# Five more w1/w3 tile pairs of each feed-forward block by seven products, and the first two w2 tiles of a third merged

## The chip, the cores and the metric

The program runs on one core of one Trainium2 chip. The metric is the device time of one execution in microseconds (us), the median of several runs.

## The reference

Two blocks follow each other on a sequence of 512 positions of width 1024, each two layers deep. The first is a hybrid attention block, the second holds feed-forward, mixer, cross-attention and again feed-forward. The change touches the feed-forward blocks alone; there are two in each of the second block's layers, so four in all:

```python
D_FF = ((8 * D_MODEL // 3) + 127) // 128 * 128          # 2816 = 22 tiles of 128

def swiglu(h, w1, w3, w2):
    return (jax.nn.silu(h @ w1) * (h @ w3)) @ w2
...
    x = x + 0.5 * swiglu(rmsnorm(x, ffn1_norm[l]), ffn1_w1[l], ffn1_w3[l], ffn1_w2[l])
...
    x = x + 0.5 * swiglu(rmsnorm(x, ffn2_norm[l]), ffn2_w1[l], ffn2_w3[l], ffn2_w2[l])
```

## The kernel before

Everything is kept transposed: channels on the 128 partitions, the 512 positions along the free axis. Each fp32 operand is split into a high part, a ScalarE copy rounded to fp32r (line L284 for weights), and a low part, VectorE's difference (L285); a product of two split operands is three matmuls on TensorE (`mm3`, L313 to L315: high by high, low by high, high by low).

A feed-forward block (`ffn`, L1059) works through its 22 hidden tiles in three thirds of 8, 7 and 7. A third has two stages.

**The pair stage.** For each hidden tile one unit computes the columns of h @ w1 and of h @ w3, applies silu and multiplies. There are two kinds of units. `gated_pair` (L917), the plain one, multiplies 16 weight blocks of 128x128 by 512 positions: 48 matmuls of 512 columns. `seven` (L951) treats the pair as a 2x2 block product over w1 and w3's halves and the positions' halves, and needs seven block products in place of eight: 7 x 4 x 3 = 84 matmuls of 256 columns. In exchange VectorE builds sums of weights (`sums`, L962), splits more weight tiles (L285: three of 1024 columns and one of 512, against two of 1024 for a plain unit), and combines the products out of PSUM (tiles `early` and `ab`, also L962). The string `PLAIN` (L33) says by a 1 which units of a third are plain.

The four weight splits of a unit of seven are called p0 to p3 in the code; the text below calls them a, s, t and d after the names under which they are kept. The products come in the order m1, m2, m6, m5, m7, m3, m4. Split s is first read by the third of them (m6), t by the fifth (m7) and d by the seventh (m4). After m4, VectorE's last add (`early<-mm,ab`) completes the unit, GpSimd multiplies by the norm's factor (L1038), ScalarE takes the silu (L1039), VectorE multiplies the halves (L1040, `sb<-early,sb`), and the result is split into `hh` and `hl` for the second stage: `hh` by ScalarE (L1073), `hl` either by VectorE (L1078, plain units and the last two of a third) or by a ScalarE copy and an accumulating DMA from GpSimd's queue (L1075, L1076).

Split weight tiles share one pool of eight buffers, so four pairs of high and low part:

```python
        return [self._new(self.sb, [P, 1040], R, "w", 8, "w" + e)[:, :n] for e in "hl"]
```

Since a unit of seven fills all four pairs, split a of the next unit waits until this unit's m2 has read its a, s until m5, t until m3, d until m4.

**The w2 stage.** For each of the 8 output tiles, one unit of `dense` multiplies the third's hidden tiles (7 or 8 blocks, three matmuls of 512 columns each) and adds into x (L1101, L1102). `go` (L408) runs the units one after another, so the first unit reads all `hh` and `hl`, that of the last hidden tile included, before the second unit starts.

The order within each engine's queue is fixed when the program is built, by a scheduler that moves instructions of later steps forward; on the chip each queue runs in that order.

Of the kernel before, what the change touches and what calls it, by code (L numbers as in the profile page):

```python
# [29 lines left out]

THIRDS = (8, 7, 7)

PLAIN = ("11100100", "0010010", "0010010")  # L33
EPS = 1e-6
BIG = 1e30
DEPTH = 2
# [1 line left out]
GRAIN = 2  # L38
# [174 lines left out]
class Prog:  # L213
# [194 lines left out]
    def go(self, units):  # L408
        for _, f in self.parts_of(units):
            f()  # L410

    def weave(self, main, fill, keep=0, lead=0):

        self.go(fill[:lead])
        fill = fill[lead:]
        tm, tf = sum(c for c, _ in main) or 1, max(1, sum(u.cost for u in fill) - keep)
        a = b = i = 0
        for c, f in self.parts_of(fill):
            while i < len(main) and a / tm <= b / tf:
                a += main[i][0]  # L420
                main[i][1]()
                i += 1
            f()
            b += c
        for _, f in main[i:]:
            f()
# [632 lines left out]
    def ffn(self, l, name, cur, nx):  # L1059
        nc, A = self.nc, self.A  # L1060
        self.run_late()
        xs = cur.xs
        r = self.norm(cur, wait=6)
        self.later(6, lambda: self.tc.keep_in_program_order(nc.scalar.preload_act_table_set("silu_and_others")))
        w13 = A[f"{name}_w13"][l]
        mv = []
        for third, nh in enumerate(THIRDS):
            hid = {}
            j0 = sum(THIRDS[:third])

            def done(j, b, added):
                hh, hl = self.s(R, "hh"), self.s(R, "hl")
                nc.scalar.activation(hh, b, AF.Copy)  # L1073
                if added:
                    nc.scalar.activation(hl, b, AF.Copy, scale=-1.0)  # L1075
                    nc.gpsimd.dma_start(out=hl, in_=b, accum_op=ALU.add)  # L1076
                else:
                    nc.vector.tensor_tensor(hl, b, hh.bitcast(F32), op=ALU.subtract)  # L1078
                hid[j] = hh, hl

            units = []
            for j in range(nh):
                flat = w13[j0 + j].rearrange("p b k c -> p (b k c)")
                if PLAIN[third][j] == "1":
                    prep, steps = self.gated_pair(flat, xs, r, lambda b, j=j: done(j, b, False))
                    if third == 0 and j < 2:

                        def operands(f, i):
                            f()
                            mv.append(self.seven_operands(xs, f"{name}_g{l}", i))  # L1090

                        for n, at in enumerate((3, 6)):
                            steps[at] = lambda f=steps[at], i=2 * j + n: operands(f, i)
                    units.append((prep, steps))
                else:
                    units.append(self.seven(flat, mv, r, lambda b, j=j: done(j, b, j < nh - 2)))

            def ev2(m, ps):

                t = self.s(nm="xr")  # L1100
                nc.vector.scalar_tensor_tensor(t, ps, 0.5, r["r"], op0=ALU.mult, op1=ALU.mult)  # L1101
                nc.vector.tensor_tensor(self.x[m], t, self.x[m], op=ALU.add)  # L1102
                if third == 2:
                    self.ready(nx, m)

            w2 = A[f"{name}_w2"][l]
            last = self.dense([w2[i][:, j0:j0 + nh] for i in range(KD)], nh, 128, hid, ev2, quick=third == 2)
            self.run_pairs(units, last[0].prep)
            self.flush()
            if third == 2:  # L1110
                self.tc.keep_in_program_order(nc.scalar.preload_act_table_set("natural_log_exp_and_others"))
            self.go(last)
            self.flush()

    def lower_bound(self):
# [475 lines left out]
```

## Time and profile before

| | |
|---|---|
| runs shown | 2951.25 us median of 3 (2950.77 to 2956.36) |
| profiled execution, its own time | 2955.5 us |
| its span, first to last instruction | 2953.7 us |
| TensorE busy | 97% of the span |
| VectorE busy | 71% |
| ScalarE busy | 50% |
| GpSimd busy | 18% |
| mean granted TensorE clock | 0.993 of full |

The profiled execution took 1.8 us more than its span, and 4.25 us more than the median of the runs shown. Busy shares are means over all stages: an engine with a low mean can still be nearly full in one of them.

### The profile page before, as it was taken

How to read it: one execution, taken by the hardware profiler on the slowest of the kernel's cores; microseconds unless marked ns; L12 is line 12 of the kernel's file. 1: busy time of each engine (PE TensorE's matmuls, PEld its weight loads, DVE VectorE, ACT ScalarE, POOL GpSimd, SP SyncE). 2: the span in 40 equal slices, each digit the busy share in tenths (PEclk: the TensorE clock that was granted, in tenths of full speed). 3: DMA queues.
4: the chain of work that ended last, by engine and by line, in shares of the span. 5: the costliest groups of instructions: out<-in, count | busy, mean ns of one | idle time of the engine just before them, and what ended most of it. 6: DMA issues, size and time to landing. Idle time of an engine off the chain costs nothing. (4 is left out here: it accounts for less than half of the span.)

```text
span 2953.7 us, 44940 instructions
## 1 busy us (share of the span) xinstructions
PE 2871.5 (97%) x17560; PEld 2425.6 (82%) x17560; DVE 2089.3 (71%) x3354; ACT 1487.6 (50%) x2406; POOL 539.1 (18%) x445
## 2 busy tenths in 40 slices
PE   8999999999999999999999999999999899999997
PEld 6777877778789887788888988888988788888896
DVE  7876578774867667785676666766767975686674
ACT  6776467774634344464453434534345554453333
POOL 3101131011111013331010112101124331100112
PEclk9999999999999999999999999999999999999999
DMA  5432234322243342232133434334342232233432
GB/s 161 130 97 83 93 97 120 86 87 92 79 118 101 107 116 89 68 124 99 64 92 101 117 99 120 93 94 122 100 118 80 79 127 87 68 94 104 117 103 69
DMA packets 95045, 294.92 MB, mean 100 GB/s; under 512 B 12832, under 2 KB 13232, under 8 KB 94832
## 3 DMA queue, kind: packets, MB, share of 16 engines
q1 hardware_dynamic: 88752, 281.26, 30.9%
q0 software_dynamic: 5792, 10.50, 2.0%
q8 instruction: 138, 2.26, 0.3%
q14 instruction: 75, 0.61, 0.1%
q10 hardware_dynamic: 288, 0.28, 0.0%
HBM read 261.46 MB, written 2.10 MB: 89 GB/s over the span
## 5 line engine op out<-in xcount | busy, mean ns | idle before, releaser
L284 ACT ACTIVATE wh<-wraw 128x1024 fp32r<-128x1024 f32 (+3 forms) x494 | 489.2, 991 | 488.8 <-PE mm L314 357.9
L313 PE MATMUL mm<-xsh,wh 128*128 128x512 f32 (+1 forms) x1856 | 699.5, 377 | 18.2 <-ACT xsh L267 11.6
L285 DVE TENSOR_TENSOR wl<-wraw,wh 128x1024 fp32r<-128x1024 f32 (+3 forms) x494 | 572.6, 1160 | 176.8 <-ACT wh L284 171.6
L314 PE MATMUL mm<-xsl,wh 128*128 128x512 f32 (+1 forms) x1856 | 685.0, 369 | 6.1 <-DVE xsl L268 6.1
L315 PE MATMUL mm<-xsh,wl 128*128 128x512 f32 (+1 forms) x1856 | 683.6, 369 | 0.0
L313 PEld LDWEIGHTS mm<-xsh,wh 128*128 128x128 f32 x1856 | 352.2, 190 | 91.1 <-ACT xsh L267 13.3
L314 PEld LDWEIGHTS mm<-xsl,wh 128*128 128x128 f32 x1856 | 352.4, 190 | 63.4 <-DVE xsl L268 8.6
L315 PEld LDWEIGHTS mm<-xsh,wl 128*128 128x128 f32 x1856 | 352.2, 190 | 62.0 <-DVE wl L285 0.3
L313 PE MATMUL mm<-hh,wh 128*128 128x512 f32 x704 | 277.9, 397 | 15.1 <-ACT hh L1073 15.1
L1038 POOL TENSOR_TENSOR sb<-early,rt 128x512 f32<-128x512 f32 x56 | 111.8, 1996 | 988.3 <-DVE early L962 938.8
L314 PE MATMUL mm<-hl,wh 128*128 128x512 f32 x704 | 278.8, 396 | 0.9 <-DVE hl L1078 0.9
L315 PE MATMUL mm<-hh,wl 128*128 128x512 f32 x704 | 276.5, 393 | 0.0
L450 POOL TENSOR_TENSOR sq<-sq,sq 128x512 f32<-128x512 f32 (+1 forms) x97 | 142.3, 1467 | 624.7 <-ACT sq L447 612.8
L284 ACT ACTIVATE wh<-sums 128x1024 fp32r<-128x1024 f32 x112 | 118.6, 1059 | 179.7 <-PE mm L314 114.3
L1101 DVE SCALAR_TENSOR_TENSOR xr<-mm,rt 128x512 f32<-128x512 f32 x96 | 66.4, 692 | 164.1 <-PE mm L315 164.0
L285 DVE TENSOR_TENSOR wl<-sums,wh 128x1024 fp32r<-128x1024 f32 x112 | 136.8, 1221 | 53.5 <-ACT wh L284 53.5
L313 PEld LDWEIGHTS mm<-hh,wh 128*128 128x128 f32 x704 | 131.7, 188 | 49.9 <-ACT hh L1073 20.3
L314 PEld LDWEIGHTS mm<-hl,wh 128*128 128x128 f32 x704 | 132.2, 188 | 34.8 <-DVE hl L1078 5.6
L315 PEld LDWEIGHTS mm<-hh,wl 128*128 128x128 f32 x704 | 132.2, 188 | 31.2
L267 ACT ACTIVATE xsh<-x,prm 128x512 fp32r<-128x512 f32 x96 | 68.8, 718 | 118.3 <-DVE x L849 35.2
L1040 DVE SCALAR_TENSOR_TENSOR sb<-early,sb 128x512 f32<-128x512 f32 x56 | 38.8, 692 | 109.7 <-ACT sb L1039 109.7
L313 PE MATMUL mm<-wh,xsh 128*128 128x256 f32 (+1 forms) x384 | 113.7, 296 | 0.0
(411 smaller groups left out, 6454.5 us busy)
## 6 DMA issues: line engine op xcount, KB each, us to landing
wraw<-in_ffn_w_dram SPq DMA_DIRECT2D x208, 512.0 KB
wraw<-in_ffn_w_dram SPq DMA_DIRECT2D x64, 448.0 KB
z<-z SPq DMA_DIRECT2D x128, 128.0 KB
wraw<-in_w_out_dram SPq DMA_DIRECT2D x32, 512.0 KB
wraw<-in_w_qk_dram SPq DMA_DIRECT2D x30, 512.0 KB
hl<-sb POOLq DMA_DIRECT2D x40, 256.0 KB, 4.5
wraw<-in_w_g_dram SPq DMA_DIRECT2D x16, 512.0 KB
wraw<-in_w_gate_dram SPq DMA_DIRECT2D x16, 512.0 KB
```

The lines of the kernel that those rows point to most:

```text
L267: self.nc.scalar.activation(hi[:, :n], src, AF.Copy, scale=g)
L284: self.nc.scalar.activation(hi, src, AF.Copy)
L285: self.nc.vector.tensor_tensor(lo, src, hi.bitcast(F32), op=ALU.subtract)
L313: self.nc.tensor.matmul(ps, ah, bh, start=first and i == 0, stop=False)
L314: self.nc.tensor.matmul(ps, ah, bl, start=False, stop=False)
L315: self.nc.tensor.matmul(ps, al, bh, start=False, stop=last and i == n - 1)
L450: (eng or self.on("acc")).tensor_tensor(acc[:, :n], acc[:, :n], sq[:, :n], op=ALU.add)
L1038: self.later(3, lambda: nc.gpsimd.tensor_tensor(g, q[:, :T], r["r"], op=ALU.mult))
L1040: self.later(5, lambda: nc.vector.scalar_tensor_tensor(g, q[:, T:], -1.0, g, op0=ALU.mult, op1=ALU.mult))
L1101: nc.vector.scalar_tensor_tensor(t, ps, 0.5, r["r"], op0=ALU.mult, op1=ALU.mult)
```

## The change

Of a block's 22 units 14 were of seven; now 19 are. Only the first three units of the first third stay plain, and the other two thirds have none. So 5 units in each of 4 blocks change kind, 20 in all. Second, `lead_in` merges the first two w2 units of every third: the blocks 0 to 5 of both come first, then the remaining block or blocks of the first, then those of the second. The weight split of the second w2 unit is called before the last steps of the pair stage are flushed.

```diff
-PLAIN = ("11100100", "0010010", "0010010")
+PLAIN = ("11100000", "0000000", "0000000")
...
+    def lead_in(self, units):
+
+        a, b = units[:2]
+
+        def prep():
+            a.prep()
+            b.prep()
+
+        cut = 6 // GRAIN
+        return [self.Unit(a.cost + b.cost, a.parts[:cut] + b.parts[:cut] + a.parts[cut:] + [self.tick] + b.parts[cut:], prep)] + units[2:]
...
             self.run_pairs(units, last[0].prep)
+            last[1].prep()
             self.flush()
...
-            self.go(last)
+            self.go(self.lead_in(last))
```

The first place is VectorE's queue in the second third of the first block, from the last add of unit 3 to the last add of unit 4, both of seven. Line numbers after the change are higher by 11 (L973 is L962 of before, L1051 is L1040). Before, the unit that follows (5) was plain:

```order
L1040 SCALAR_TENSOR_TENSOR sb_2402_9692<-early_2389_9617,sb_2402_9692 128x512
L285 TENSOR_TENSOR wl_2414_9752<-wraw_2412_9749,wh_2413_9751 128x1024
L962 TENSOR_TENSOR early_2411_9746<-mm_2410_9720,cd_2409_9717 128x2x256
L962 TENSOR_TENSOR sums_2432_9870<-wraw_2426_9845 128x512
L962 TENSOR_TENSOR sums_2436_9891<-wraw_2425_9843,wraw_2426_9845 128x512
L285 TENSOR_TENSOR wl_2421_9790<-wraw_2419_9787,wh_2420_9789 128x1024
L962 TENSOR_TENSOR ab_2416_9781<-aux_2415_9755,early_2411_9746 128x512
L962 TENSOR_TENSOR sums_2432_9870<-sums_2432_9870,wraw_2425_9843 128x512
L962 TENSOR_TENSOR early_2411_9746<-aux_2415_9755,ab_2416_9781 128x256
L285 TENSOR_TENSOR wl_2428_9848<-wraw_2425_9843,wh_2427_9847 128x1024
```

Now it is of seven, and so is the one behind it:

```order
L973 TENSOR_TENSOR sums_2447_9946<-wraw_2434_9871,wraw_2435_9873 128x512
L973 TENSOR_TENSOR sums_2447_9946<-sums_2442_9911,wraw_2434_9871 128x512
L285 TENSOR_TENSOR wl_2437_9876<-wraw_2434_9871,wh_2436_9875 128x1024
L973 TENSOR_TENSOR early_2433_9868<-mm_2432_9842,cd_2431_9839 128x2x256
L1051 SCALAR_TENSOR_TENSOR sb_2424_9814<-early_2411_9737,sb_2424_9814 128x512
L285 TENSOR_TENSOR wl_2444_9915<-sums_2442_9911,wh_2443_9914 128x1024
L973 TENSOR_TENSOR ab_2439_9905<-aux_2438_9879,early_2433_9868 128x512
L973 TENSOR_TENSOR sums_2464_10042<-wraw_2457_10004 128x512
L973 TENSOR_TENSOR early_2433_9868<-aux_2438_9879,ab_2439_9905 128x256
L973 TENSOR_TENSOR sums_2464_10042<-sums_2464_10042,wraw_2456_10002 128x512
L285 TENSOR_TENSOR wl_2449_9950<-sums_2447_9946,wh_2448_9949 128x1024
L285 TENSOR_TENSOR wl_2451_9954<-wraw_2435_9873,wh_2450_9953 128x512
```

Between the same two adds there are now two half sums of unit 5 first (`sums_2447`), then splits and combining adds as before, and among them the two first half sums of unit 6 (`sums_2464`) and a fourth split; the multiplication behind the silu (`sb_2424`) has moved from the head of the piece to the fifth row.

The second place is TensorE's queue where the w2 stage of the same third begins. `mm_2459` is the first w2 unit's bank and `mm_2463` the second's; `hh_2454` and `hl_2455` are the last hidden tile. Before:

```order
L315 MATMUL mm_2459_10030<-hh_2449_9971,wl_2447_9955 128x512
L313 MATMUL mm_2459_10030<-hh_2454_10020,wh_2446_9954 128x512
L313 MATMUL mm_2463_10058<-hh_2362_9450,wh_2457_10026 128x512
L314 MATMUL mm_2459_10030<-hl_2455_10021,wh_2446_9954 128x512
L315 MATMUL mm_2459_10030<-hh_2454_10020,wl_2447_9955 128x512
L314 MATMUL mm_2463_10058<-hl_2363_9451,wh_2457_10026 128x512
L315 MATMUL mm_2463_10058<-hh_2362_9450,wl_2458_10027 128x512
L313 MATMUL mm_2463_10058<-hh_2375_9533,wh_2457_10026 128x512
L314 MATMUL mm_2463_10058<-hl_2376_9534,wh_2457_10026 128x512
```

Now, with `mm_2495` the first unit's bank, `mm_2496` the second's, and `hh_2490` and `hl_2491` the last hidden tile:

```order
L313 MATMUL mm_2496_10237<-hh_2483_10166,wh_2488_10200 128x512
L314 MATMUL mm_2496_10237<-hl_2484_10167,wh_2488_10200 128x512
L315 MATMUL mm_2496_10237<-hh_2483_10166,wl_2489_10201 128x512
L313 MATMUL mm_2495_10218<-hh_2490_10208,wh_2479_10135 128x512
L314 MATMUL mm_2495_10218<-hl_2491_10209,wh_2479_10135 128x512
L315 MATMUL mm_2495_10218<-hh_2490_10208,wl_2480_10136 128x512
L313 MATMUL mm_2496_10237<-hh_2490_10208,wh_2488_10200 128x512
L314 MATMUL mm_2496_10237<-hl_2491_10209,wh_2488_10200 128x512
L315 MATMUL mm_2496_10237<-hh_2490_10208,wl_2489_10201 128x512
```

The last hidden tile was read by the 19th matmul of the stage; now 36 matmuls on the other six tiles come ahead of it.

## Rows read from the trace of the kernel before

**Rows 1.** The page, busy us of each engine (share of the span), then its instructions.
```profile
PE 2871.5 (97%) x17560; PEld 2425.6 (82%) x17560; DVE 2089.3 (71%) x3354; ACT 1487.6 (50%) x2406; POOL 539.1 (18%) x445
```

**Rows 2.** Three stretches; busy us of each engine (instructions), PEclk is the clock share.
```profile
1010.45:1020.34 9.89, 9.89 (x85) 9.89 (x84) 6.16 (x9) 4.17 (x5) 0.00 (x0) 1.00 0.33 106
1020.34:1030.23 9.89, 9.89 (x87) 9.89 (x85) 7.50 (x10) 5.66 (x8) 2.16 (x2) 1.00 0.37 102
1030.23:1041.40 11.17, 11.17 (x51) 9.04 (x50) 9.02 (x14) 4.33 (x7) 3.67 (x2) 1.00 0.53 143
```

**Rows 3.** Timeline of PE, ends of two thirds: start us, us, then the instruction.
```profile
857.72 0.50 PE L313 MATMUL mm<-hh,wh 128*128 128x512 f32 x1 [1.12 <-ACT hh L1073]
858.45 0.51 PE L314 MATMUL mm<-hl,wh 128*128 128x512 f32 x1 [0.23 <-DVE hl L1078]
...
1085.91 0.40 PE L315 MATMUL mm<-hh,wl 128*128 128x512 f32 x1
1087.65 0.73 PE L313 MATMUL mm<-hh,wh 128*128 128x512 f32 x2 [1.34 <-ACT hh L1073]
...
1088.94 0.39 PE L314 MATMUL mm<-hl,wh 128*128 128x512 f32 x1
```

**Rows 4.** Timelines of ACT and DVE in the stretch's first unit.
```profile
1016.23 1.07 ACT L284 ACTIVATE wh<-sums 128x1024 fp32r<-128x1024 f32 x1 [1.79 <-PE aux L314]
1019.06 1.06 ACT L284 ACTIVATE wh<-sums 128x1024 fp32r<-128x1024 f32 x1 [1.76 <-PE mm L314]
...
1014.48 1.23 DVE L285 TENSOR_TENSOR wl<-wraw,wh 128x1024 fp32r<-128x1024 f32 x1 [1.94 <-ACT wh L284]
...
1017.33 1.22 DVE L285 TENSOR_TENSOR wl<-sums,wh 128x1024 fp32r<-128x1024 f32 x1 [1.02 <-ACT wh L284]
```

**Rows 5.** Timeline of DVE where it never waits.
```profile
1030.34 0.68 DVE L962 TENSOR_TENSOR sums<-sums,wraw 128x512 f32<-128x512 f32 x1
1030.94 0.41 DVE L962 TENSOR_TENSOR early<-aux,ab 128x256 f32<-128x256 f32 x1
1031.28 1.21 DVE L285 TENSOR_TENSOR wl<-wraw,wh 128x1024 fp32r<-128x1024 f32 x1
1032.41 0.68 DVE L962 TENSOR_TENSOR early<-mm,ab 128x512 f32<-128x512 f32 x1
```

**Rows 6.** Timelines of DVE, POOL and ACT behind two units' last adds.
```profile
1021.89 0.68 DVE L962 TENSOR_TENSOR early<-mm,ab 128x512 f32<-128x512 f32 x1
1024.71 0.69 DVE L1040 SCALAR_TENSOR_TENSOR sb<-early,sb 128x512 f32<-128x512 f32 x1 [2.13 <-ACT sb L1039]
1025.66 1.23 DVE L285 TENSOR_TENSOR wl<-wraw,wh 128x1024 fp32r<-128x1024 f32 x1 [0.26 <-ACT wh L284]
...
1022.72 1.29 POOL L1038 TENSOR_TENSOR sb<-early,rt 128x512 f32<-128x512 f32 x1 [49.58 <-DVE early L962]
...
1033.18 2.79 POOL L1038 TENSOR_TENSOR sb<-early,rt 128x512 f32<-128x512 f32 x1 [5.34 <-DVE early L962]
...
1024.04 0.63 ACT L1039 ACTIVATE sb<-sb 128x512 f32<-128x512 f32 x1 [1.71 <-POOL sb L1038]
1024.58 1.05 ACT L284 ACTIVATE wh<-wraw 128x1024 fp32r<-128x1024 f32 x1
...
1034.14 0.68 DVE L962 TENSOR_TENSOR sums<-sums,wraw 128x512 f32<-128x512 f32 x1
```

**Rows 7.** Timeline of DVE at a third's end.
```profile
1082.71 0.68 DVE L962 TENSOR_TENSOR early<-mm,ab 128x512 f32<-128x512 f32 x1
...
1087.63 0.69 DVE L1078 TENSOR_TENSOR hl<-sb,hh 128x512 fp32r<-128x512 f32 x1 [0.69 <-ACT hh L1073]
```

**Rows 8.** Two lines of the program: min/median/max of an instruction, and of a DMA's landing.
```profile
L1101 DVE SCALAR_TENSOR_TENSOR xr<-mm,rt x96: 677/692/695, 859.2 to 2936.1; 128x512 f32<-128x512 f32 x96
...
DMA to landing us min/median/max: 3.2/4.5/6.2
```

## The prediction

> **What bounds the kernel now.** I read the page first: TensorE is busy 97% of the span, VectorE 71% [rows 1], so TensorE sets the time and the other engines count only where it waits for them. Then the pair stage in windows. A unit of seven takes TensorE 9.89 us, twice in a row, at full clock, and a plain unit 11.17 us [rows 2]; the busy time equals the window each time, so nothing is waited for there. VectorE is busy 6.2, 7.5 and 9.0 of these: the wait-free window in which it is fullest is the plain one, where it works for the units of seven on either side.
>
> Then the ends of the thirds in TensorE's timeline. The w2 stage runs 18 matmuls and stops for the last hidden tile, first for `hh`, then briefly for `hl`: the profile books 1.34 us in a third of seven, 1.12 and 0.23 in the third of eight [rows 3]. The whole loss is longer, since the matmuls behind also come late. At 11.17/48 = 0.233 us per matmul the fifth one behind that of 1085.91 was due at 1087.08; it came at 1088.94 [rows 3]. So about 1.87 us at each of the 12 ends, 22.4 us in all.
>
> **What the change takes from TensorE.** 20 units go from 11.17 to 9.89: 20 x 1.28 = 25.6 us. The merge puts 36 matmuls (8.38 us) ahead of the first one that reads the last `hh`, where 18 (4.19 us) stood. If nothing else moved, that would cover the whole 1.87 us each time.
>
> **What it adds to VectorE, and who waits.** In the run where VectorE never waits [rows 5], the start of the next instruction comes 0.60 us after a 512-column add's, 0.34 after one of 256 and 1.13 after a 1024-column split's. In a long run of sevens each unit costs 3 x 1.13 + 0.60 for splits, 4 x 0.60 for sums, 3 x 0.60 + 0.34 for combining and 0.60 for the last multiplication: 9.1 us, under TensorE's 9.89. On means alone VectorE keeps up. But its queue is in order and holds three waits, so I follow it, with the lag: how long after a unit's last matmul its last add (`early<-mm,ab`) starts.
>
> Before, unit 0 of the second third ended at 1020.34 [rows 2] and its last add started at 1021.89: lag 1.55 [rows 6]. In that unit split s began at 1017.33, 6.88 us in, because its ScalarE half had to wait for m5 to free a buffer (1016.23) [rows 4]. Now two half sums for unit 2 stand in that unit as well. From the start of split s to the last add the queue then holds s, a combining add, a sum, the 256-column add, a sum, t and d: 1.13 + 0.60 + 0.60 + 0.34 + 0.60 + 1.13 + 0.60 = 5.0. So the lag after unit 0 is 6.88 + 5.0 - 9.89 = 2.0.
>
> Behind the last add stand two more sums, split a, the next unit's first combining add, and then the multiplication by the silu, which needs GpSimd's product first. That product is the price to settle. With VectorE idle it took 1.29 us; with VectorE at work it took 2.79 (1033.18 to 1035.97), which is 1.15 us after VectorE's `sums` of 1034.14 had ended at 1034.82 [rows 6]. So GpSimd makes next to no headway beside VectorE's splits and sums, which read two operands in SBUF. VectorE's adds out of PSUM seem not to collide: L1101 stayed within 677 to 695 ns in all 96 cases [rows 8]. I take it that GpSimd starts when VectorE comes to the combining add; bounds: it runs freely at once, or it must wait for that add too (0.60 us later).
>
> The Trainium skill says the same in general ("SBUF — State Buffer", section "SBUF: two separate sides"): VectorE and GpSimd share a pair of ports under an exclusive lock, and a VectorE instruction with two SBUF inputs keeps GpSimd out entirely. It speaks against this change, and the trace agrees, 2.79 against 1.29 us.
>
> The loop from one last add to the next, with 2.93 us (0.60 + 0.60 + 0.60 + 1.13) until the combining add: GpSimd ends at 3.02 + 1.15 = 4.17; silu starts at 4.2 and ScalarE's half of s 0.54 later, ends 1.05 after that (the steps 1024.04, 1024.58, 1025.63 [rows 6]); VectorE's s at 5.8, and the last add 5.0 later: 10.8 us. That is 0.95 longer than the unit, so the lag grows by 0.95 per unit. Only behind unit 0 is it less, as split a is not ready before 4.03 us into the unit (1014.48 [rows 4]) and GpSimd gets in ahead of it: 5.03 + 1.13 + 0.60 + 0.60 + 5.0 gives a lag of 2.5. So after units 0 to 4: 2.0, 2.5, 3.4, 4.4, 5.3. Unit 5 has no sums to make for a unit 7 (-1.2, and 0.1 back for an add that follows its operand directly): 5.2.
>
> **Does TensorE wait in the run?** Split s of a unit is done 7.05 us after the lag's add, and is read by the third product, 9.89 + 2.83 = 12.72 us after TensorE began the unit before. At a lag of 5.3 it is there at 12.35: just in time. Split t is done at 9.5 + 5.3 = 14.8 and is wanted at 9.89 + 5.65 = 15.5. So no wait, with 0.4 us to spare at the worst place. VectorE's load is hidden by a lead of one unit, and that lead is nearly eaten up at the end of a run of seven; without it each such unit would cost 10.8 us.
>
> **The ends of the thirds.** From unit 5's last add, with GpSimd free: silu's multiplication after 2.82 (1021.89 to 1024.71 [rows 6]); then three w2 splits of 896 columns (1.0 us each, between 0.60 and 1.13), a ScalarE half of 0.85 ahead of the first, two combining adds, the 256-column one and an `hl`, together 6.1. The last unit's add comes 8.9 after that of unit 5: lag 5.2 + 8.9 - 9.89 = 4.2 us. Before it was 0.8: the stage began 18 matmuls ahead of 1086.14, at 1081.95, and the add at 1082.71 [rows 3, 7]. From there the chain to TensorE's first `hh` matmul was 1087.65 - 1082.71 = 4.94 us (the same rows), to `hl` 1087.63 + 0.69 + 0.06 - 1082.71 = 5.67. Now `hl` is ready at 4.2 + 5.67 = 9.9 us into the w2 stage, and TensorE wants it after 37 matmuls, at 8.6: it still loses 1.3 us, and the merge earns 0.55 there, 8 times: 4.4. In the first third the run has only five units: lags 2.0, 2.5, 3.4, 3.3 and 2.7 at the end (splits of 1024); `hl` at 8.4 to 8.5, no loss, 4 x 1.87 = 7.5.
>
> The 12 more results that go through GpSimd's accumulating DMA cost nothing: the latest is issued some 10 us before TensorE wants it, and such a DMA lands within 6.2 us [rows 8]. The weights read from HBM stay the same.
>
> **Sum.** 25.6 + 7.5 + 4.4 = 37.5 us off. Against the profiled execution's own 2955.5 us that is 2918; on the median of the runs shown, 4.25 us lower, 2914. That is the forecast.
>
> **Rivals.** (A) The forecast: VectorE lags, TensorE is not held up in the runs, some of the end waits stay. (B) GpSimd is not kept out, or gets in between two instructions: then the lag stays near 2, all end waits go, 25.6 + 22.4 = 48 us off: 2903. For it: VectorE's 9.1 is under 9.89. Against: 2.79 against 1.29. (C) The lag grows faster, by the other bound 1.55 per unit: 2.0, 2.5, 4.0, 5.6, 7.1; split s then comes about 2 us late near the end of the eight long runs and the last `hl` stays 1 us later than I have it. Of 33 us that leaves some 10 to 25 off: 2926 to 2941. (D) Slower than before: VectorE's loop becomes the pace. At 10.8 us, 7 units take 75.6 against 5 x 9.89 + 2 x 11.17 = 71.8, and 5 take 54.0 against 50.7: 8 x 3.8 + 4 x 3.3 = 44 us more, less at most 22.4 from the ends, so about 2973. It decides when a unit's s or t is wanted from the first units on, that is if the lead of one unit is not there; with the lead (some 4 us in each of 12 runs, 40 loops in all) it takes a loop of 9.89 + (25.6 + 48)/40 = 11.7 us. The windows of 9.89 us with no wait speak against it. (E) The end waits stay as they were, and only the units pay: 25.6 off, 2926.
>
> **How the numbers follow.** A 0.45, B 0.2, C 0.15, E 0.12, D 0.05, others 0.03. The predicted time is A's, 2914. A by itself runs from 2909 to 2919. The range reaches to B at the lower end and a little past E and into C at the upper: 2902 to 2932. A measurement tells about 0.2% (6 us) from no change; D and the far end of C are all that could reach that: faster 0.92, same 0.03, slower 0.05.
>
> **What would show it.** Right: TensorE's units of seven at 9.89 us everywhere in the runs; GpSimd's product (then L1049) longer than 2 us behind most units, ending 1.15 us after a split; VectorE's last add later behind each unit of a third, up to about 5 us; waits for `hl` gone in the first thirds and near 1 us in the others. Wrong: waits of TensorE for a weight split inside a run (C or D), end waits of nil in all thirds (B) or of 2 us (E).

## The result and the profile after

The changed kernel took 2913.07 us (median of 4 runs, 2910.57 to 2917.41), the kernel before 2951.43 us in the same series (2950.77 to 2956.36). The ratio is 0.9864, with a 95% interval of 0.9852 to 0.9875: 38 us faster. The forecast was 2914.

The profiled execution took 2911.61 us. Its page, first part (busy time, share of the span, instructions), stands against [rows 1]:

```profile
PE 2841.3 (98%) x18280; PEld 2443.4 (84%) x18280; DVE 2212.5 (76%) x3522; ACT 1522.5 (52%) x2478; POOL 619.0 (21%) x477
```

TensorE is busy for less time, at a higher share. Next the windows of the last third of the first feed-forward block, one line for each of its seven units (start and end in us, length, then the busy time of TensorE, its weight loads, VectorE, ScalarE and GpSimd, and the granted clock):

```profile
1004.00:1013.83 9.83, 9.83 (x85) 9.82 (x84) 6.70 (x10) 4.20 (x5) 0.00 (x0) 1.00 0.34 108
1013.83:1023.65 9.82, 9.82 (x86) 9.82 (x85) 9.82 (x13) 6.00 (x8) 2.50 (x2) 1.00 0.34 108
1023.65:1033.47 9.82, 9.82 (x86) 9.82 (x85) 8.31 (x12) 5.25 (x8) 3.58 (x2) 1.00 0.47 133
1033.47:1043.29 9.82, 9.82 (x86) 9.82 (x85) 8.31 (x13) 4.52 (x8) 3.99 (x2) 1.00 0.47 135
1043.29:1053.11 9.82, 9.82 (x86) 9.82 (x85) 8.57 (x13) 4.40 (x7) 4.28 (x2) 1.00 0.43 112
1053.11:1062.93 9.82, 9.82 (x86) 9.82 (x85) 8.89 (x13) 4.30 (x8) 4.27 (x2) 1.00 0.42 98
1062.93:1072.75 9.82, 9.82 (x86) 9.82 (x85) 6.73 (x9) 6.54 (x11) 2.16 (x2) 1.00 0.44 115
```

TensorE waits for nothing in the run: seven units of 9.82 us where [rows 2] had 9.89 and 11.17. VectorE's timeline of the same stretch shows how far it falls behind. The lines are the last add behind each unit, one `sums` and one split (start, duration):

```profile
1015.86 0.69 DVE L973 TENSOR_TENSOR early<-mm,ab 128x512 f32<-128x512 f32 x1
...
1017.06 1.79 DVE L973 TENSOR_TENSOR sums<-sums,wraw 128x512 f32<-128x512 f32 x1
...
1026.11 0.68 DVE L973 TENSOR_TENSOR early<-mm,ab 128x512 f32<-128x512 f32 x1
...
1027.91 1.22 DVE L285 TENSOR_TENSOR wl<-wraw,wh 128x1024 fp32r<-128x1024 f32 x1
...
1036.95 0.68 DVE L973 TENSOR_TENSOR early<-mm,ab 128x512 f32<-128x512 f32 x1
...
1047.79 0.69 DVE L973 TENSOR_TENSOR early<-mm,ab 128x512 f32<-128x512 f32 x1
...
1058.63 0.69 DVE L973 TENSOR_TENSOR early<-mm,ab 128x512 f32<-128x512 f32 x1
...
1068.39 0.68 DVE L973 TENSOR_TENSOR early<-mm,ab 128x512 f32<-128x512 f32 x1
...
1077.26 0.69 DVE L973 TENSOR_TENSOR early<-mm,ab 128x512 f32<-128x512 f32 x1
```

The start of each last add less the end of its window is the lag: 2.03, 2.46, 3.48, 4.50, 5.52, 5.46, 4.51. Forecast were 2.0, 2.5, 3.4, 4.4, 5.3, 5.2, 4.2. GpSimd's timeline gives the reason, its product in that stretch:

```profile
1016.68 1.62 POOL L1049 TENSOR_TENSOR sb<-early,rt 128x512 f32<-128x512 f32 x1 [45.99 <-issue]
...
1026.94 3.34 POOL L1049 TENSOR_TENSOR sb<-early,rt 128x512 f32<-128x512 f32 x1 [3.39 <-PE mm L315]
...
1059.42 3.39 POOL L1049 TENSOR_TENSOR sb<-early,rt 128x512 f32<-128x512 f32 x1 [3.61 <-DVE early L973]
...
1069.17 1.28 POOL L1049 TENSOR_TENSOR sb<-early,rt 128x512 f32<-128x512 f32 x1 [2.53 <-DVE early L973]
```

The same multiplication takes 1.28 us beside an idle VectorE, 3.34 to 3.40 when VectorE's two sums and a split go first, and 1.62 when GpSimd gets in between two of VectorE's instructions. Then it is VectorE that stands still: the `sums` of 1017.06 took 1.79 us in place of the usual 0.68. In the whole trace 29 of the 76 products took 3.3 to 3.4 us and 20 took 1.6 to 1.7; exactly 20 `sums` took 1.8 us. Three more, of 2.2 us, got in one `sums` later, ahead of split a, and there the split took 2.1 us in place of 1.2. The other 24 stand behind the last two units of the runs, where no `sums` follow.

Last, TensorE at the start of the w2 stage of this third, which began at 1072.76, against [rows 3]:

```profile
1080.91 0.39 PE L315 MATMUL mm<-hh,wl 128*128 128x512 f32 x1
1082.20 0.49 PE L313 MATMUL mm<-hh,wh 128*128 128x512 f32 x1 [0.90 <-ACT hh L1084]
1082.93 0.50 PE L314 MATMUL mm<-hl,wh 128*128 128x512 f32 x1 [0.23 <-DVE hl L1089]
```

It now runs 36 matmuls, 8.4 us, before it wants the last `hh`, and still waits 1.55 us in all (1.06 for `hh`, 0.49 for `hl`). This is the worst end: six of the eight long thirds wait about 0.5 us for `hl` (two of them 0.1 for `hh` too), one hardly at all, and the four thirds of eight not at all.

### The profile page after: what moved, and what is told of

It reads as the page before. It is cut to its first block, busy times and chain, and to the rows that moved or that the text cites. A ratio compares the mean times of both kernels' runs of the same rounds, so it can differ in the third digit from the quotient of the medians.

```text
span 2909.8 us, 46900 instructions
## 1 busy us (share of the span) xinstructions
PE 2841.3 (98%) x18280; PEld 2443.4 (84%) x18280; DVE 2212.5 (76%) x3522; ACT 1522.5 (52%) x2478; POOL 619.0 (21%) x477
## 5 line engine op out<-in xcount | busy, mean ns | idle before, releaser
L313 PE MATMUL mm<-xsh,wh 128*128 128x512 f32 (+1 forms) x1696 | 618.6, 365 | 17.4 <-ACT xsh L267 11.1
L314 PE MATMUL mm<-xsl,wh 128*128 128x512 f32 (+1 forms) x1696 | 603.5, 356 | 6.7 <-DVE xsl L268 6.7
L315 PE MATMUL mm<-xsh,wl 128*128 128x512 f32 (+1 forms) x1696 | 602.6, 356 | 0.8 <-DVE wl L285 0.8
L314 PEld LDWEIGHTS mm<-xsl,wh 128*128 128x128 f32 x1696 | 322.6, 190 | 49.7 <-DVE xsl L268 8.1
L315 PEld LDWEIGHTS mm<-xsh,wl 128*128 128x128 f32 x1696 | 322.1, 190 | 48.6 <-DVE wl L285 1.2
L1049 POOL TENSOR_TENSOR sb<-early,rt 128x512 f32<-128x512 f32 x76 | 177.6, 2336 | 818.5 <-DVE early L973 606.3
L284 ACT ACTIVATE wh<-sums 128x1024 fp32r<-128x1024 f32 x152 | 160.1, 1053 | 121.5 <-PE mm L314 93.3
L285 DVE TENSOR_TENSOR wl<-sums,wh 128x1024 fp32r<-128x1024 f32 x152 | 185.4, 1220 | 20.8 <-ACT wh L284 20.8
L1050 ACT ACTIVATE sb<-sb 128x512 f32<-128x512 f32 x76 | 48.1, 633 | 232.2 <-POOL sb L1049 232.2
L973 DVE TENSOR_TENSOR sums<-sums,wraw 128x512 f32<-128x512 f32 x152 | 126.0, 829 | 0.5
```

Of the source, the lines that this page charges most:

```text
L284: self.nc.scalar.activation(hi, src, AF.Copy)
L285: self.nc.vector.tensor_tensor(lo, src, hi.bitcast(F32), op=ALU.subtract)
L313: self.nc.tensor.matmul(ps, ah, bh, start=first and i == 0, stop=False)
L314: self.nc.tensor.matmul(ps, ah, bl, start=False, stop=False)
L315: self.nc.tensor.matmul(ps, al, bh, start=False, stop=last and i == n - 1)
L973: add = lambda o, a, b: nc.vector.tensor_tensor(o, a, b, op=ALU.add)
```

## The experiments

e1 to e9 are nine kernels. All were profiled, so the span of each can be cut into three: the pair stages of the eight thirds of seven, the twelve w2 stages, and everything else (the pair stages of the thirds of eight stand in this part). The table is worked out from the starts of TensorE's matmuls; a w2 stage runs from its first matmul to the first one behind it. All in us.

```
kernel                      pairs of 7   w2     the rest   span     median
before                      572.6        512.1  1869.1     2953.7   2951.4
the change                  552.6        495.5  1861.7     2909.8   2913.1
e1 table alone              552.6        554.9  1862.8     2970.2   2973.7
e2 merge alone              572.6        489.8  1867.2     2929.6   2933.4
e3 product on VectorE       552.6        489.8  1864.5     2906.9   2908.0
e4 a quarter of the product 552.6        489.8  1863.5     2905.8   2907.3
e5 product twice            593.2        543.7  1866.9     3003.7   3007.1
e6 e3, 20 units of seven    553.7        489.8  1861.5     2905.0   2906.8
e7 e3 without the merge     552.6        491.8  1860.7     2905.1   2909.3
e8 the change, a line less  552.6        493.2  1866.2     2912.0   2913.0
e9 before, with e3's edit   572.6        492.1  1873.6     2938.3   2939.0
```

489.8 is a w2 part with no wait in it. The rest holds the pair stages of the thirds of eight (together 301.6 us before and 296.7 in the change, from the norm's last `aux` matmul to the w2 stage) and all that lies outside the feed-forward blocks. No edit touches the latter, yet it took between 1564.3 and 1571.9 us in these eleven traces; e9 shows what differs. By time alone, what less than 4 us separates isn't told apart here.

### e1: the table alone

The theory behind the forecast says that VectorE's lag, grown over a long run, comes out at the end of the third. Without the merge it must cost more than the units bring. The rival says that the end costs what it cost.

```diff
-            last[1].prep()
...
-            self.go(self.lead_in(last))
+            self.go(last)
```

> The table of the change alone: 19 units of seven, but the two w2 units of a third stay one behind the other and the second one's split stays where it was. Theory (VectorE's last add comes later behind each unit of a run, by 0.95 us a unit, because GpSimd's product waits for VectorE): the last lag of a long run is 3.4 to 4.5 us as in the trace of the change, hl is ready 5.7 us after that, 9.1 to 10.2 us into the w2 stage, and is wanted after 19 matmuls, at 4.4: 4.7 to 5.8 us lost at each of 8 ends, about 3.5 to 4 at the 4 ends of the thirds of eight, 52 to 62 in all where the kernel before loses 22. The units give 25.6. So about 2951 - 25.6 + 30 to 40: slower than before, 2955 to 2967, and 42 to 54 us over the whole change. Rival (the last chain of a third is as long as before, only the units count): 2926.

Measured: 2973.72 us, ratio to before 1.007 (1.0058 to 1.0083). **Slower than before by 20 us**, and by 61 than the change. The w2 part is 59.4 us above that of the change. That is 65 us more than without a wait, where 52 to 62 were expected; the total is 7 us beyond its range. The timeline of TensorE at the end of the last third of the first block shows why:

```profile
1086.88 0.39 PE L315 MATMUL mm<-hh,wl 128*128 128x512 f32 x1
1091.72 1.22 PE L313 MATMUL mm<-hh,wh 128*128 128x512 f32 x2 [4.46 <-ACT hh L1084]
1092.74 0.63 PE L314 MATMUL mm<-hl,wh 128*128 128x512 f32 x1
1093.17 0.63 PE L315 MATMUL mm<-hh,wl 128*128 128x512 f32 x1
...
1094.75 0.40 PE L314 MATMUL mm<-hl,wh 128*128 128x512 f32 x1
1094.98 0.39 PE L315 MATMUL mm<-hh,wl 128*128 128x512 f32 x1
```

Behind the wait the matmuls come 0.43 us apart, then 0.23 again. The windows of this stretch (the number behind GpSimd's is the granted clock):

```profile
1082.92:1087.20 4.28, 4.28 (x20) 3.20 (x18) 4.25 (x7) 1.67 (x2) 0.00 (x0) 1.00 0.66 173
1087.20:1091.70 4.50, 0.06 (x1) 0.00 (x0) 2.00 (x3) 1.27 (x3) 2.04 (x1) 0.94 0.78 229
1091.70:1096.00 4.30, 4.28 (x13) 3.39 (x14) 2.82 (x4) 2.93 (x4) 0.00 (x0) 0.67 0.04 14
```

The granted clock went from full to a mean of 0.67: the lower level (1.2 of 2.4 GHz), then full again. Five matmuls ran at the lower level here, and 77 in the twelve w2 stages of e1, each 0.2 us late: 15 us that the expectation hadn't counted. Without them the ends lose 50 us, a little less than the theory has.

### e2: the merge alone

```diff
-PLAIN = ("11100000", "0000000", "0000000")
+PLAIN = ("11100100", "0010010", "0010010")
```

> The merge alone: the table of before, the first two w2 units merged, the second one's split ahead of the last flush. Theory: with short runs of sevens the last lag stays 0.8 us, hl is ready some 6.5 to 7.5 us into the w2 stage (the second split goes ahead of it on VectorE) and is wanted after 37 matmuls, at 8.6: all 12 end waits of 1.87 us go, 22.4 us off, 2929 (2926 to 2932). Rival (the ends cost what they cost whatever stands ahead of them): 2951.

Measured: 2933.44 us, ratio 0.9931 (0.9918 to 0.9945). The w2 part falls from 512.1 to 489.8, by 22.3 us where 22.4 were expected; the median falls by 19.7 and lies 1.4 us above the range. Together with e1: the table alone costs 20 us, the merge alone brings 20, both bring 38. Neither part's worth can be read from it alone.

### e3: the product on VectorE

```diff
-            self.later(2, lambda: add(q[:, H:3 * H], st["y2"], st["v"]))
-            self.later(3, lambda: nc.gpsimd.tensor_tensor(g, q[:, :T], r["r"], op=ALU.mult))
+
+            def end():
+                add(q[:, H:3 * H], st["y2"], st["v"])
+                nc.vector.tensor_tensor(g, q[:, :T], r["r"], op=ALU.mult)
+
+            self.later(2, end)
```

> The whole change, with the multiplication by r moved from GpSimd to VectorE, right behind the last add. Theory: VectorE then has 9.7 us of work in a unit of 9.89 but no longer waits for GpSimd in its queue; the lag stays at 2.0 to 2.2 us behind every unit of a run, split s starts when ScalarE's half lets it, and the last waits at the w2 stages (about 5 us in all in the trace of the change) go: 2907 to 2910, 3 to 6 us under the change. Rival (VectorE's own work is what makes the lag grow, so that 0.6 us more of it a unit makes it worse): lags over 5 us at the end of a run and a time at or above that of the change, 2913 to 2925.

Measured: 2908.03 us, ratio 0.9843 (0.983 to 0.9857), as the theory has it. This interval still touches that of the change; the w2 part, 489.8 against 495.5, and the lags tell the two apart. VectorE's last adds in the third of seven units (timeline, first three and the last), and its busy time in the second unit (windows):

```profile
1013.60 0.69 DVE L973 TENSOR_TENSOR early<-mm,ab 128x512 f32<-128x512 f32 x1
1023.42 0.69 DVE L973 TENSOR_TENSOR early<-mm,ab 128x512 f32<-128x512 f32 x1
1033.25 0.69 DVE L973 TENSOR_TENSOR early<-mm,ab 128x512 f32<-128x512 f32 x1
...
1071.20 0.69 DVE L973 TENSOR_TENSOR early<-mm,ab 128x512 f32<-128x512 f32 x1
```

```profile
1011.58:1021.40 9.82, 9.82 (x87) 9.82 (x86) 9.82 (x15) 5.98 (x8) 0.86 (x1) 1.00 0.33 110
```

The adds come every 9.82 us, TensorE's own pace: the lag stays at 2.02 to 2.04 (1023.42 less 1021.40) and is 0.7 at the end. VectorE is busy for the whole unit, since instructions overlap by 0.08 us, and nothing waits. So it isn't the amount of VectorE's work that makes the lag grow, but what it waits for. This edit takes out both GpSimd's own time and the time that it is kept out; which of them counts is read from the trace of the change, below.

### e4: a quarter of the product

The product by r is done for 128 of 512 columns; the other 384 go into the silu without the factor.

```diff
-            self.later(3, lambda: nc.gpsimd.tensor_tensor(g, q[:, :T], r["r"], op=ALU.mult))
-            self.later(4, lambda: nc.scalar.activation(g, g, AF.Silu))
+            self.later(3, lambda: nc.gpsimd.tensor_tensor(q[:, :P], q[:, :P], r["r"][:, :P], op=ALU.mult))
+            self.later(4, lambda: nc.scalar.activation(g, q[:, :T], AF.Silu))
```

> The whole change, with GpSimd's multiplication by r done for 128 of the 512 columns alone (the rest of the product is left out and goes to the silu without it), at the same place. Theory (VectorE's sums and splits keep GpSimd out until they end): the product's time hardly falls with its size, from 3.35 us to some 2.4 to 2.7 behind most units, ending shortly after VectorE's split; the lag grows by 0.1 to 0.3 us a unit. Rival (both go on side by side and GpSimd is only slower, about 2.6 times): a quarter of the columns takes a quarter of the time, 0.8 to 1.0 us, and the lag doesn't grow at all. Time in both cases some us under the change, 2907 to 2912, as the end waits shrink.

Measured: 2907.25 us, ratio 0.9841 (0.9828 to 0.9854). The edit did more than was meant: these 128 columns are complete with the first combining add already, and the scheduler put the product there, ahead of the last add and off the loop. So the lags of 2.0 to 2.3 prove nothing. The durations do tell the two theories apart. From the timelines of GpSimd and VectorE:

```profile
1009.33 0.46 POOL L1049 TENSOR_TENSOR early<-early,rt 128x128 f32<-128x128 f32 x1 [48.23 <-DVE early L973]
...
1029.68 1.83 POOL L1049 TENSOR_TENSOR early<-early,rt 128x128 f32<-128x128 f32 x1
```

```profile
1029.86 1.35 DVE L285 TENSOR_TENSOR wl<-sums,wh 128x1024 fp32r<-128x1024 f32 x1 [0.53 <-ACT wh L284]
```

Alone it takes 0.46 us. Where VectorE begins a split 0.18 us later, it takes 1.83 and ends 0.30 behind the split; 50 of the 76 took 1.8. The delay is the length of VectorE's instruction, not a multiple of GpSimd's own: the two take turns, and the rival's 0.8 to 1.0 is out. The theory's 2.4 to 2.7 wasn't met either, as the product now meets one split and no `sums`. By the profile's starts the split won these turns although GpSimd's instruction had begun 0.1 to 0.3 us before it, on an idle VectorE, in all 50 cases.

### e5: the product twice

```diff
+            self.later(3, lambda: nc.gpsimd.tensor_tensor(g, q[:, :T], r["r"], op=ALU.mult))
             self.later(3, lambda: nc.gpsimd.tensor_tensor(g, q[:, :T], r["r"], op=ALU.mult))
```

> The whole change, with GpSimd's multiplication by r done twice behind each unit of seven (the second time over the first, with the same result). Theory: VectorE's queue stands still until the silu, so GpSimd's second pass runs alone and adds 1.28 us to the loop from one last add to the next: some 12.1 us against TensorE's 9.89. The lag then grows by up to 2.2 us a unit, passes the 5.7 us at which the third product of the next unit has to wait for split s by the third or fourth unit of a run, and TensorE waits inside the runs from there on, 5 to 9 us in each long run and 2 to 4 in each short one, the last waits included: 2950 to 2985, that is, as slow as before the change or slower. Rival (the lead of one unit takes it up, and only the last waits grow by 1.3 us each): 2920 to 2930, and no wait of TensorE inside a run.

Measured: 3007.07 us, ratio 1.018 (1.0163 to 1.0197), beyond both ranges. The windows of the fifth and sixth unit of a long run (the four ahead of them took 9.82 us):

```profile
938.09:949.20 11.11, 10.11 (x87) 9.90 (x86) 11.08 (x15) 5.42 (x8) 4.01 (x3) 1.00 0.39 119
949.20:961.37 12.17, 10.65 (x87) 10.03 (x86) 9.32 (x13) 5.31 (x8) 5.53 (x4) 1.00 0.37 97
```

From the fifth unit on TensorE waits: 11.1, 12.2 and 11.8 us a unit here, 10.9 to 12.2 in all long runs, where a loop of 12.1 was worked out. That is 5.1 us in each long run and 1.0 in each short one. Expected were 5 to 9 and 2 to 4, the last waits included, and these come on top: the w2 part is 48 us above that of the change, 4 us at each end. The last lag is 4.7 to 5.4 us in all twelve runs, the last unit's product is done twice as well, which the expectation left out, and 55 of the matmuls run at the lower clock. In this run the first wait isn't for split s, as worked out, but for split a; so it is in nine of the twelve runs, and in the other three it is for split s. VectorE's and GpSimd's timelines and TensorE's wait:

```profile
934.21 0.68 DVE L973 TENSOR_TENSOR early<-mm,ab 128x512 f32<-128x512 f32 x1
...
935.41 1.78 DVE L973 TENSOR_TENSOR sums<-sums,wraw 128x512 f32<-128x512 f32 x1
937.12 2.31 DVE L285 TENSOR_TENSOR wl<-wraw,wh 128x1024 fp32r<-128x1024 f32 x1
```

```profile
935.05 1.60 POOL L1049 TENSOR_TENSOR sb<-early,rt 128x512 f32<-128x512 f32 x1 [3.67 <-DVE early L973]
936.73 1.62 POOL L1050 TENSOR_TENSOR sb<-early,rt 128x512 f32<-128x512 f32 x1
```

```profile
939.48 0.39 PE L315 MATMUL pt<-xsh,wl 128*128 128x256 f32 x1 [1.00 <-DVE wl L285]
```

GpSimd got in twice. The `sums` took 1.1 us more and split a (the `wl` of 937.12) 1.1 more, each about as long as GpSimd held it up.

### e6: 20 units of seven

On e3, the third unit of the first third by seven products as well:

```diff
-PLAIN = ("11100000", "0000000", "0000000")
+PLAIN = ("11000000", "0000000", "0000000")
```

> The product on VectorE as in e3, and 20 instead of 19 of the 22 pairs by seven products (the third unit of the first third too): 4 more units at 9.89 instead of 11.17. Theory (VectorE keeps up with 9.7 us a unit, lags of 2.0): 5.1 us off e3, 2901 to 2905. Rival: the unit's operands from x are made in the two units ahead of it on VectorE, and its sums and splits now fall there as well, so TensorE waits at its start, 1 to 3 us each time, and most of the gain goes: 2905 to 2910.

Measured: 2906.78 us, ratio 0.9837 (0.9822 to 0.9852), the lowest median of all, within the rival's range and not told apart from e3 (2908.03). What the rival would have, a wait at the unit's start, isn't there: the pair stage of the first third is 1.2 us shorter in each block, as the theory has it of one unit (from the norm's last `aux` matmul to the w2 stage 73.4 against 74.6 us in three blocks, 71.4 against 72.6 in the first). The two long runs of the first block took 0.5 us more each. What is left, some 4 us, is less than the spread outside the feed-forward blocks.

### e7: e3 without the merge

e3 with the edit of e1.

> The product on VectorE as in e3, 19 units of seven, but without the merge of the two w2 units (as in e1). Theory: what the missing merge costs is set by the last lag. With 0.7 to 0.95 us, as in e3 and before the change, hh is ready 5.7 us into the w2 stage and wanted at 4.2: the old 1.87 us at each of 12 ends, 22 us over e3, 2927 to 2933, and some 43 us under e1. Rival (19 units of seven need the merge whatever the lag): 2965 to 2975.

Measured: 2909.32 us, ratio 0.9846 (0.9832 to 0.9861). **The expectation was wrong**, and so was the rival: the w2 part is 491.8, only 2.0 us above that of e3 with the merge. The timelines of VectorE (last add), ScalarE (`hh`) and TensorE at the end of the last third of the first block, whose w2 stage starts with the first line of TensorE's:

```profile
1071.14 0.69 DVE L973 TENSOR_TENSOR early<-mm,ab 128x512 f32<-128x512 f32 x1
```

```profile
1074.85 0.63 ACT L1088 ACTIVATE hh<-sb 128x512 fp32r<-128x512 f32 x1 [0.76 <-DVE sb L1055]
```

```profile
1070.43 0.40 PE L313 MATMUL mm<-hh,wh 128*128 128x512 f32 x1
...
1075.08 0.39 PE L315 MATMUL mm<-hh,wl 128*128 128x512 f32 x1
1075.31 0.72 PE L313 MATMUL mm<-hh,wh 128*128 128x512 f32 x2
```

`hh` is there at 1075.48, 5.05 us into the stage and 4.34 behind the last add; in the kernel before, TensorE's first matmul on it came 4.94 behind [rows 3, 7]. And TensorE doesn't want it after 18 matmuls any more: with this edit the scheduler put four matmuls of the next w2 unit ahead, so that 22 x 0.233 = 5.1 us pass first. Half a microsecond less of chain and four matmuls more of cover were nearly all that the old end wait lacked.

### e8: one line less

The line `last[1].prep()` was taken out of the change.

> The whole change but for one line: the split of the second w2 unit's weights is asked for behind the last flush, so it stands on ScalarE and VectorE behind the last unit's chain. Theory: VectorE's queue is in order, the split comes after hl, 10 us into the w2 stage, and TensorE wants those weights after 18 matmuls, at 4.2: some 5 to 6 us lost at each end in place of the 0.5 us, as much as without the merge or more, 2968 to 2990. Rival (the split slips in while the chain waits for GpSimd and the silu, and hl comes 1 us sooner for it): 2908 to 2914.

Measured: 2913.02 us, ratio 0.986 (0.9845 to 0.9875). The expectation took the place in the code for the place in the queue: the scheduler makes the same order on every engine with or without this line, so e8 is the change once more, and the line does nothing. It shows one thing: the last third of the first block, 40.66 us of w2 stage in the trace of the change, took 39.51 in this one. Which products GpSimd gets in early isn't fixed by the program.

### e9: the kernel before, with the product on VectorE

e3's edit on the kernel before, to test what e7 suggests.

> The kernel before, table and w2 stage untouched, with one edit: the multiplication by r on VectorE right behind the last add, in place of GpSimd. The program's own scheduler then puts 22 matmuls ahead of the first that reads the last hh in a third of seven, where it put 18 (4 of them from the next w2 unit, in the order of TensorE's instructions as it is compiled). Theory (from e7: the end waits are lost when the last hh comes sooner by some 0.55 us and four more matmuls stand ahead of it): hh is ready at 0.8 + 4.35 = 5.1 us, wanted at 22 x 0.233 = 5.1, so the end waits of 20.4 us in the trace of before go without any merge: 2932 (2929 to 2936), like the merge alone in e2. Rival (in e7 it was the run of sevens ahead that made the end waits go, or the time was won elsewhere): the ends keep most of their 1.7 us each, 2945 to 2954.

Measured: 2938.96 us, ratio 0.9942 (0.9929 to 0.9956). The w2 part falls to 492.1, by 20.0 us where 20.4 were expected: the theory holds for the ends. The median falls by 15 only and lies 3 us above the range; the profiled execution was the longest of its five, and its rest is 4.5 us longer than that of before. These 4.5 us arise at three places outside the feed-forward blocks (near 90, 1165 and 2360 us), behind which the same matmul comes 1.7, 1.3 and 1.4 us later than in the trace of before. At each of them the granted clock, whose mean in a window is the number behind GpSimd's, spent longer at its lower level in this execution. The windows of the first two, before:

```profile
80.00:100.00 20.00, 18.19 (x136) 16.06 (x134) 19.65 (x51) 17.94 (x42) 5.92 (x4) 1.00 0.34 114
1155.00:1175.00 20.00, 17.34 (x215) 13.06 (x214) 18.23 (x43) 9.39 (x17) 7.38 (x11) 1.00 0.17 54
```

and in e9:

```profile
80.00:100.00 20.00, 18.18 (x128) 16.79 (x126) 18.58 (x47) 16.51 (x39) 5.93 (x4) 0.91 0.34 113
1155.00:1175.00 20.00, 17.34 (x210) 13.41 (x208) 18.14 (x44) 9.05 (x16) 4.14 (x6) 0.91 0.20 59
```

The times fit: of the five executions the one with a mean granted clock of 0.993, as in the trace of before, took 2933.74 us, inside the expected range; the three at 0.991 took 2938.96 to 2940.34. Why the clock fell more often in them isn't shown.

## Why the prediction was right

**The units.** 25.6 us were forecast for 20 units. Measured: 20.0 for 16 in the long thirds (572.6 less 552.6) and 1.1 to 1.4 each, together 4.9, for the four in the thirds of eight, 24.8 in all.

**The lag and the lock.** The growth of 0.95 us a unit, its cause and its place were right. Behind 1036.95 to 1058.63 it is 1.02 a unit, in the other blocks 0.93 to 0.96, and the product of 1026.94 ended at 1030.28, 1.15 us behind the split that kept it out, as forecast. e3 shows the cause: without GpSimd in the loop no lag grows, though VectorE has more to do. e4 shows that it is turns, not shared speed. The step held only half of the mechanism: "VectorE's splits and sums keep GpSimd out" is as true the other way round. The Trainium skill ("SBUF — State Buffer", section "SBUF: two separate sides") says that whichever of the two starts first has the ports for its whole instruction, and the prediction used only one side of that. The 20 `sums` of 1.8 us agree. But the 29 products of 3.3 to 3.4 us, which had begun 0.4 us ahead of the second `sums`, and the 50 of e4 don't: by the profile's starts the first one there can still come last. Where GpSimd gets in, a unit adds 0.36 to 0.44 to the lag, not 0.95; so some 0.4 is what GpSimd's place in the loop costs even then, and the other 0.6 comes of its being kept out. Behind unit 0 the small step was forecast, since GpSimd would get in ahead of split a; the size came in all twelve runs, that way of it in three, and in nine it got in ahead of a `sums`.

**No wait in the runs.** Right, at lags up to 5.5. The bound itself, 5.7, is not tested. In e5 TensorE's first wait comes in the unit after next behind a lag of 5.95 (934.21 less 928.26), but it is for split a, and in two of the runs whose first wait is for split s it comes behind a lag of 5.5: there GpSimd's second pass also lengthens the way from the last add to the splits.

**The ends.** This term was mis-sized: 11.9 us were forecast, 16.6 came (512.1 less 495.5). The first thirds lost nothing, as forecast. The long ones were to lose 1.3 us each, on a last lag of 4.2; the lag was 2.9 to 3.6 in seven of the eight, as GpSimd got in early at least once behind units 1 to 4 of each, and 4.5 in the one shown above, where it never did. The mean lag is 3.5, 0.7 less than forecast, and the mean loss 0.7, 0.6 less. The formula stands: at 4.5 it gives 1.6, and the trace shows 1.55.

**The sum.** By the traces 24.8 + 16.6 = 41.4 us against 37.5; the rest gave 2.5 more, and the profiled executions differ by 43.9. The medians differ by 38.4. That the forecast came within 1 us of the median is partly luck: the term that was 4.7 short is hidden by the spread between executions, which goes with the granted clock. Of the changed kernel's four, the two with a mean clock of 0.993 and 0.994 took 2911.61 and 2910.57 us, the two at 0.991 took 2914.53 and 2917.41.

**The rivals.** B (GpSimd gets in between two instructions) was a case in part: of the 40 loops that were forecast to keep GpSimd out, 11 let it in and 29 didn't. D's turning point of 11.7 us agrees with e5, whose loop of some 12 makes it slower than the kernel before; but more than half of e5's loss lies in the w2 stages. E (the end waits stay) is not what happened, and e1, the table without the merge, is much worse than it: the end waits can't stay as they were when the lag grows. What I didn't see is how cheaply they could be had. I priced the merge as the way to cover them, and e7 and e9 show that moving one 0.6 us multiplication off GpSimd covers nearly all.

## What to carry to other kernels

An in-order engine that waits for a helper in its own loop can fall behind by a fixed amount per unit, when the loop is longer than the unit, without the pacing engine waiting; follow the lag through the run to the first place where its result is wanted, because that place, not the run, pays. A cheap product that is moved to an idle engine can cost more than on the busy one, if the two take turns at a port. And two edits that meet in one wait must be measured alone and together: here one cost 20 us, the other brought 20, and both brought 38.

## What the runs showed of the hardware

The turns between VectorE and GpSimd go either way, with the same instructions at the same distance: GpSimd's start lay 0.22 to 0.23 us behind that of a `sums` both for a product of 1.62 us (1016.68, above) and for one of 3.34 (1026.94). These are the two `sums` in VectorE's timeline of the change:

```profile
1016.46 0.68 DVE L973 TENSOR_TENSOR sums<-wraw,wraw 128x512 f32<-128x512 f32 x1
...
1026.71 0.68 DVE L973 TENSOR_TENSOR sums<-wraw,wraw 128x512 f32<-128x512 f32 x1
```

What decides is open.

Behind the 24 waits of 2.4 to 4.6 us at the w2 stages of e1 and e5 TensorE's clock fell to its lower level 19 times, for 4 to 12 matmuls; behind the 12 of up to 1.5 us of the kernel before it never did. This makes a long wait dearer than its length.
